# Mixer output projection: one accumulation over eight feature tiles in place of six and then two

## The chip, the core and the metric

The kernel runs on one core of a Trainium2 chip. Its time is the time of one launch on the device, in microseconds (us). The core has a matrix engine (TensorE, "PE" in the profile), an engine for elementwise work on two tensors (VectorE, "DVE"), one for functions of one tensor (ScalarE, "ACT"), a slower elementwise engine (GpSimd, "POOL") and one that issues the transfers (SyncE, "SP"). Each engine works through its own queue in order; engines wait for each other by semaphores.

## The reference, cut to what matters

One decoder layer over 1,024 prompt tokens and 32 sample tokens, 1,056 in all, all in float32. The part that matters here stands between the mixer and the second feed-forward block:

```python
merged = (sigmoid(gate_s5) * (y_s5 @ w_s5_up) + sigmoid(gate_m) * (hm @ w_m_up))
x = x + merged @ w_out                                   # w_out is 1024 x 1024
x = x + 0.5 * swiglu(rmsnorm(x, g_ffn2), w2_gate, w2_up, w2_down)
```

## The kernel before

Activations lie with features on the 128 partitions and the 1,056 tokens along the row, so a tensor of 1,024 features is eight tiles of 128 x 1056, numbered 0 to 7. Tokens go in three column pieces, `CH`: 384, 384 and 288. Float32 accuracy is had by splitting each operand into a high and a low part and multiplying three times (high by high, high by low, low by high: `mm3`, lines 109 to 111). `split` (lines 92 and 93) makes the parts: a copy on ACT gives the high one, a subtraction on DVE the low one. `weight` loads a block of weights (line 100) and splits it; `unit` accumulates one output piece of 128 x 384 or 128 x 288 over a list of feature tiles in one bank of PSUM, of which the tag "mm" has four.

`join` first makes the eight merged tiles `mg` (high and low, sixteen tiles), from the products `mm_mu`. Then comes the output projection `mm_wo`, which the change touches. It runs in two passes: for each of the eight output tiles, a product over the feature tiles 0 to 5, added to the residual tile `x` by `piece` (line 1297, on DVE); and then, again for each output tile, a product over the feature tiles 6 and 7, added in the same way. Only behind the second of these is a tile of `x` complete, and `hook(m)` is called.

The hook is that of `norm_s`. It prepares the second feed-forward block and has this work:

- for every tile of `x`, three squares on ACT (lines 339 and 342) and their sum on DVE (line 343, into `rb_n`);
- for every second tile, `build`: a store of the two tiles of `x` to DRAM (line 332), scaled copies `n3na` and `n3nb` on ACT (lines 326 to 328), four sums on POOL (`forms`, lines 135 to 138, written over the two tiles of `x`), and seven splits into the forms `n3b11`, `n3t3`, `n3t2`, `n3t1`, `n3b21`, `n3t4`, `n3nb22` of a fast matrix multiplication (`sproducts`): seven copies on ACT and seven subtractions on DVE. The program has four builds, 0 to 3;
- behind the last tile, for each of the three column pieces, `rstd`: a product `nps_n` on PE, a few tiny operations on DVE with a power on POOL (line 305) between them, a product `nrb_n` on PE, and a copy on ACT.

After this the feed-forward block starts. Its products `mma` and `mmd` can be run up to a point while the hook's work is going on; `mmb` (line 183) stands in PE's queue behind the last `nrb_n`. From `mmb` on PE is kept busy.

Two stores of tiles matter. All tiles of 128 x 1056, `x`, `mg` and the seven forms of each build among them, come from one pool of 34 slots (tag "s"); a tile whose slot isn't free yet waits for the last reader of the one that held it. `n3na` and `n3nb` come from a pool of two. The split weights come from a pool of eight (tag "w"), four pairs.

Nothing in the kernel fixes the order of the queues, apart from a few loads that are pinned: a scheduler orders each engine's instructions when the program is built, by priority and by its own estimate of when things become ready.

Of the kernel before, what the change touches and what calls it, by code (L numbers as in the profile page):

```python
# [10 lines left out]
ALU = mybir.AluOpType  # L11
# [4 lines left out]
P = 128  # L16
# [3 lines left out]
KT = 8  # L20
# [10 lines left out]
CH = ((0, 384), (384, 384), (768, 288))  # L31
# [4 lines left out]
class Kernel:  # L36
# [1237 lines left out]
    def join(self, hook):  # L1274

        nc, v, a = self.nc, self.nc.vector, self.a
        hm = self.hm
        mg = self.new_hl(2, "mg") + self.new_hl(4, "mg2", "x") + [tuple(self.ph.tile([P, NT], F32R, tag="s", name=f"mg{q}{k}") for q in "hl") for k in (6, 7)]
        for m in range(KT):
            w = self.weight(a["w_m_up"][0][:, m * P:(m + 1) * P], f"mu{m}")  # L1280
            tm = self.pr.tile([P, RW], F32, tag="r", name=f"jm{m}")[:, :NT]
            self.pinned_load(tm, self.d_tm[m])
            for j, (o, n) in enumerate(CH):
                ps = self.unit(w, hm, j, f"mu{m}_{j}")
                t = self.pt.tile([P, 384], F32, tag="h", name=f"mg{m}_{j}")[:, :n]
                v.scalar_tensor_tensor(t, tm[:, o:o + n], 1.0, ps, op0=ALU.add, op1=ALU.mult)
                v.tensor_tensor(t, t, self.a5[m][:, o:o + n], ALU.add)
                self.split(t, mg[m][0][:, o:o + n], mg[m][1][:, o:o + n])
        self.x = [self.pa.tile([P, NT], F32, tag="s", name=f"x2_{m}") for m in range(KT)]
        for m in range(KT):  # L1290
            self.pinned_load(self.x[m], self.d_x[m])

        def piece(w, ks, m, c, j):
            o, n = CH[j]
            ps = self.unit(w, ks, j, f"wo{m}_{j}_{len(ks)}", c)
            xs = self.x[m][:, o:o + n]
            v.scalar_tensor_tensor(xs, ps, 0.25, xs, op0=ALU.mult, op1=ALU.add)
        wo = a["w_out"][0]
        for m in range(KT):
            w = self.weight(wo[:6 * P, m * P:(m + 1) * P], f"wo{m}")  # L1300
            for j in range(3):
                piece(w, mg[:6], m, 0, j)
        ws = [self.weight(wo[6 * P:, 512 * i:512 * i + 512], f"wo_{i}") for i in range(2)]
        for m in range(KT):
            for j in range(3):
                piece(ws[m // 4], mg[6:], m, m % 4, j)
            hook(m)


# [140 lines left out]
```

## Time and profile before

| | us |
|---|---|
| median of three runs | 2322.53 |
| lowest and highest run | 2320.86, 2325.98 |
| the profiled execution | 2326.38 |
| its span, first to last instruction | 2324.7 |

The span is what the trace shows, and all positions below are microseconds from its start. The profiled execution took 1.7 us more than its span. PE is busy for 2252.8 us of it. The output projection, with the hook's work behind it, lies from about 1535 to 1673 us. Names in the trace leave the numbers of tiles out, so `x` stands for any of the eight tiles.

### The profile page before, as it was taken

How to read it: one execution, taken by the hardware profiler on the slowest of the kernel's cores; microseconds unless marked ns; L12 is line 12 of the kernel's file. 1: busy time of each engine (PE TensorE's matmuls, PEld its weight loads, DVE VectorE, ACT ScalarE, POOL GpSimd, SP SyncE). 2: the span in 40 equal slices, each digit the busy share in tenths (PEclk: the TensorE clock that was granted, in tenths of full speed). 3: DMA queues.
4: the chain of work that ended last, by engine and by line, in shares of the span. 5: the costliest groups of instructions: out<-in, count | busy, mean ns of one | idle time of the engine just before them, and what ended most of it. 6: DMA issues, size and time to landing. Idle time of an engine off the chain costs nothing.

```text
span 2324.7 us, 39749 instructions
## 1 busy us (share of the span) xinstructions
PE 2252.8 (97%) x15663; PEld 2206.2 (95%) x15663; DVE 1394.2 (60%) x3211; ACT 823.7 (35%) x1560; POOL 549.1 (24%) x570
## 2 busy tenths in 40 slices
PE   5999999999999999999999999999699999999999
PEld 4899999999999999999999889999599999999998
DVE  5655555335858867769676476535755555523754
ACT  6433333113424433444344252213533333311543
POOL 4676664000001100000000000002576766100000
PEclk8899999999999999999999999999799999999999
DMA  5122226421444542122124676232123222722101
GB/s 196 56 74 67 82 74 198 145 74 46 142 122 121 138 136 60 53 65 63 52 60 128 179 269 251 84 130 75 51 74 92 74 77 91 252 72 69 56 19 75
DMA packets 283492, 240.48 MB, mean 103 GB/s; under 512 B 28652, under 2 KB 260044, under 8 KB 283304
## 3 DMA queue, kind: packets, MB, share of 16 engines
q1 hardware_dynamic: 264064, 216.34, 30.2%
q10 hardware_dynamic: 19240, 21.59, 2.8%
q8 instruction: 123, 2.02, 0.4%
q14 instruction: 65, 0.53, 0.1%
HBM read 168.04 MB, written 67.35 MB: 101 GB/s over the span
## 4 chain that ended last, share of the span: by engine, by line
PE 88%; DVE 6%; DMA 2%; issue 1%; ACT 1%; POOL 1%; SPq 1%; DVEq 0%; ACTq 0%; POOLq 0%
PE mm_qk L110 3%; PE mm_qk L109 3%; PE mm_qk L111 3%; PE mm_f2d L110 2%; PE mm_f1d L110 2%; PE mm_f2d L111 2%; PE mm_f1d L111 2%; PE mm_f2d L109 2%; PE mm_f1d L109 2%; PE mmc_f2g L183 2%; PE mmc_f2u L183 2%; PE mmd_f2u L183 2%; PE mmd_f1u L183 2%; PE mma_f2u L183 2%; PE mma_f1u L183 2%; PE mmc_f1u L183 2%
## 5 line engine op out<-in xcount | busy, mean ns | idle before, releaser
L109 PE MATMUL mm_qk<-n2h,wh_qk 128*128 128x384 f32 (+1 forms) x384 | 125.9, 328 | 0.0
L110 PE MATMUL mm_qk<-n2l,wh_qk 128*128 128x384 f32 (+1 forms) x384 | 125.8, 327 | 0.0
L109 PE MATMUL mm_f1d<-f1hh,wh_f1d 128*128 128x384 f32 (+1 forms) x384 | 122.8, 326 | 2.6 <-DVE x_f L415 1.5
L111 PE MATMUL mm_qk<-n2h,wl_qk 128*128 128x384 f32 (+1 forms) x384 | 125.3, 326 | 0.0
L110 PE MATMUL mm_f1d<-f1hl,wh_f1d 128*128 128x384 f32 (+1 forms) x384 | 124.6, 325 | 0.4 <-DVE f1hl L93 0.4
L109 PE MATMUL mm_f2d<-f2hh,wh_f2d 128*128 128x384 f32 (+1 forms) x384 | 123.1, 326 | 1.8 <-ACT f2hh L92 1.5
L110 PE MATMUL mm_f2d<-f2hl,wh_f2d 128*128 128x384 f32 (+1 forms) x384 | 124.0, 324 | 0.7 <-DVE f2hl L93 0.7
L111 PE MATMUL mm_f1d<-f1hh,wl_f1d 128*128 128x384 f32 (+1 forms) x384 | 124.5, 325 | 0.0
L111 PE MATMUL mm_f2d<-f2hh,wl_f2d 128*128 128x384 f32 (+1 forms) x384 | 123.5, 322 | 0.0
L1014 POOL TENSOR_TENSOR cy<-cs,mhalf 128x1 f32<-128x1 f32 x32 | 20.3, 635 | 431.4 <-DVE cs L1013 408.4
L305 POOL TENSOR_TENSOR rc_n<-nv_n,mhalf 128x3 f32<-128x3 f32 x12 | 13.5, 1126 | 425.8 <-DVE nv_n L301 397.1
L415 DVE SCALAR_TENSOR_TENSOR x_f<-mm_f1d,x_f 128x384 f32<-128x384 f32 (+1 forms) x72 | 37.0, 520 | 88.0 <-PE mm_f1d L111 87.7
L956 DVE SCALAR_TENSOR_TENSOR cv<-raw,vecs,cv 128x384 f32<-128x384 f32 (+1 forms) x144 | 84.8, 589 | 7.3 <-ACT cv L954 6.1
L415 DVE SCALAR_TENSOR_TENSOR x_f<-mm_f2d,x_f 128x384 f32<-128x384 f32 (+1 forms) x72 | 37.1, 520 | 85.6 <-PE mm_f2d L111 85.6
L158 POOL TENSOR_TENSOR wr_f2g<-wr_f2g,wr_f2g 128x512 f32<-128x512 f32 x16 | 20.6, 1287 | 242.9 <-DVE wa_f2g L93 233.7
L109 PEld LDWEIGHTS mm_f1d<-f1hh,wh_f1d 128*128 128x128 f32 x384 | 72.4, 189 | 3.3 <-DVE x_f L415 1.7
L109 PEld LDWEIGHTS mm_f2d<-f2hh,wh_f2d 128*128 128x128 f32 x384 | 71.7, 188 | 2.9 <-ACT f2hh L92 2.1
L110 PEld LDWEIGHTS mm_f2d<-f2hl,wh_f2d 128*128 128x128 f32 x384 | 72.1, 188 | 1.3 <-DVE f2hl L93 1.3
L110 PEld LDWEIGHTS mm_f1d<-f1hl,wh_f1d 128*128 128x128 f32 x384 | 72.7, 189 | 0.6 <-DVE f1hl L93 0.6
L111 PEld LDWEIGHTS mm_f1d<-f1hh,wl_f1d 128*128 128x128 f32 x384 | 72.7, 189 | 0.0
L110 PEld LDWEIGHTS mm_qk<-n2l,wh_qk 128*128 128x128 f32 x384 | 72.3, 188 | 0.1
L111 PEld LDWEIGHTS mm_qk<-n2h,wl_qk 128*128 128x128 f32 x384 | 72.2, 188 | 0.1
(728 smaller groups left out, 7501.2 us busy)
## 6 DMA issues: line engine op xcount, KB each, us to landing
d_xs<-x SPq DMA_DIRECT2D x16, 528.0 KB
d_f1h<-f1h SPq DMA_DIRECT2D x16, 528.0 KB
f1hr<-d_f1h SPq DMA_DIRECT2D x16, 528.0 KB
x_f<-d_xs SPq DMA_DIRECT2D x16, 528.0 KB
d_f2h<-f2h SPq DMA_DIRECT2D x16, 528.0 KB
f2hr<-d_f2h SPq DMA_DIRECT2D x16, 528.0 KB
wr_f1g<-in_w_gate_dram SPq DMA_DIRECT2D x16, 512.0 KB
wr_f1u<-in_w_up_dram SPq DMA_DIRECT2D x16, 512.0 KB
```

What stands on the lines that cost most here:

```text
L109: mm(ps, wh, xh, start=start, stop=False)
L110: mm(ps, wh, xl, start=False, stop=False)
L111: mm(ps, wl, xh, start=False, stop=stop)
L158: g.tensor_tensor(src, src, add, ALU.add)
L183: nc.tensor.matmul(ps, w[:, wq, i], f[q][:, xq, cs], start=start and i == j == 0, stop=i == n - 1 and j == 2, skip_group_check=not start)
L305: nc.gpsimd.tensor_tensor(r, ms, self.mhalf[:, :nt], ALU.pow)
L415: v.scalar_tensor_tensor(xs, ps, 0.5, xs, op0=ALU.mult, op1=ALU.add)
L956: v.scalar_tensor_tensor(acc, raw[:, o + i:o + i + wd], self.cw[:, i, T:T + 1], acc, op0=ALU.mult, op1=ALU.add)
L1014: nc.gpsimd.tensor_tensor(y, ss, self.mhalf[:n, 0:1], ALU.pow)
```

## The change

The two passes become one: for each output tile, a weight block of all 1,024 rows is loaded and split, one product runs over all eight feature tiles, one update adds it to `x`, and the hook is called at once.

```diff
         for m in range(KT):
-            w = self.weight(wo[:6 * P, m * P:(m + 1) * P], f"wo{m}")
-            for j in range(3):
-                piece(w, mg[:6], m, 0, j)
-        ws = [self.weight(wo[6 * P:, 512 * i:512 * i + 512], f"wo_{i}") for i in range(2)]
-        for m in range(KT):
-            for j in range(3):
-                piece(ws[m // 4], mg[6:], m, m % 4, j)
+            w = self.weight(a["w_out"][0][:, m * P:(m + 1) * P], f"wo{m}")
+            for j, (o, n) in enumerate(CH):
+                ps = self.unit(w, mg, j, f"wo{m}_{j}")
+                xs = self.x[m][:, o:o + n]
+                v.scalar_tensor_tensor(xs, ps, 0.25, xs, op0=ALU.mult, op1=ALU.add)
             hook(m)
```

The number of matrix products stays as it was (8 x 3 x 8 x 3). Updates of `x` go from 48 to 24, weight blocks from ten (eight of 128 x 768, two of 128 x 1024) to eight of 128 x 1024. The scheduler orders everything from here to the start of the feed-forward block anew.

On ACT, before the change, all weight blocks of the projection (`wh_wo`) and the first four of the feed-forward block stand ahead of the first square of the hook (`rb_n3` from `x2_0`):

```order
L92 ACTIVATE wh_wo3_16997<-wr_wo3_16995 128x768
L92 ACTIVATE mgh7_15995<-mg7_2_16776 128x288
L92 ACTIVATE wh_wo4_17063<-wr_wo4_17061 128x768
L92 ACTIVATE wh_wo5_17129<-wr_wo5_17127 128x768
L92 ACTIVATE wh_wo6_17195<-wr_wo6_17193 128x768
L92 ACTIVATE wh_wo7_17261<-wr_wo7_17259 128x768
L92 ACTIVATE wh_wo_0_17327<-wr_wo_0_17325 128x1024
L92 ACTIVATE wh_wo_1_17333<-wr_wo_1_17331 128x1024
```

Now, at the same place of ACT's queue, the hook of tile 0 stands between the weight blocks 3 and 5:

```order
L92 ACTIVATE wh_wo3_17104<-wr_wo3_17102 128x1024
L92 ACTIVATE mgh7_15995<-mg7_2_16776 128x288
L339 ACTIVATE rb_n3_15979<-x2_0_16781 128x384
L339 ACTIVATE rb_n3_15979<-x2_0_16781 128x384
L92 ACTIVATE wh_wo4_17229<-wr_wo4_17227 128x1024
L339 ACTIVATE rb_n3_15979<-x2_0_16781 128x288
L326 ACTIVATE n3na_0_16979<-x2_0_16781,vecs_144 128x1056
L92 ACTIVATE n3b11_0_16988<-n3na_0_16979 128x528
```

The hook's ACT work for the tiles 0 to 6 is spread in this way over the whole projection.

Later in ACT's queue, where the last output tile (7) is made, now stand the seven copies of build 2 between the squares of tile 7, and behind them the first scaled copy of build 3 (`n3na_3`):

```order
L342 ACTIVATE sq_n30_7_17622<-x2_7_16788 128x384
L92 ACTIVATE n3b11_2_17424<-n3na_2_17415 128x528
L92 ACTIVATE n3t3_2_17427<-x2_5_16786 128x528
L92 ACTIVATE n3t2_2_17430<-x2_4_16785 128x528
L342 ACTIVATE sq_n31_7_17625<-x2_7_16788 128x384
L92 ACTIVATE n3t1_2_17433<-x2_4_16785 128x528
L92 ACTIVATE n3b21_2_17436<-n3nb_2_17416 128x528
L92 ACTIVATE n3t4_2_17439<-x2_5_16786 128x528
L92 ACTIVATE n3nb22_2_17442<-n3nb_2_17416 128x528
L326 ACTIVATE n3na_3_17633<-x2_6_16787,vecs_144 128x1056
```

These seven tiles take the slots of `mg` tiles: the program gives them the addresses of the high and low parts of the feature tiles 0 to 3. The builds 0 and 1 lie ahead of this, in slots that were free or held finished tiles of `x`.

On POOL, behind the last output tile, the rows of build 3 (`x2_6`, `x2_7`) and of the powers (`rc_n3`) before the change had one sum of feed-forward weights (`wr0_f2u0`, line 158) among them:

```order
L305 TENSOR_TENSOR rc_n3_15980<-nv_n30_17724,mhalf_88 128x3
L135 TENSOR_TENSOR x2_7_16788<-n3na_3_17693,n3nb_3_17694 128x528
L137 TENSOR_TENSOR x2_6_16787<-n3nb_3_17694,x2_6_16787 128x528
L158 TENSOR_TENSOR wr0_f2u0_18034<-wr0_f2u0_18034,wr1_f2u0_18036 128x4x128
L138 TENSOR_TENSOR x2_7_16788<-n3nb_3_17694,x2_6_16787 128x528
L305 TENSOR_TENSOR rc_n3_15980<-nv_n31_17741,mhalf_88 128x3
L305 TENSOR_TENSOR rc_n3_15980<-nv_n32_17758,mhalf_88 128x3
```

Now three stand there, and the power of the second column piece (`nv_n31`) ahead of the last sum:

```order
L305 TENSOR_TENSOR rc_n3_15980<-nv_n30_17664,mhalf_88 128x3
L136 TENSOR_TENSOR x2_6_16787<-n3na_3_17633 128x528
L158 TENSOR_TENSOR wr0_f2u0_17974<-wr0_f2u0_17974,wr1_f2u0_17976 128x4x128
L135 TENSOR_TENSOR x2_7_16788<-n3na_3_17633,n3nb_3_17634 128x528
L137 TENSOR_TENSOR x2_6_16787<-n3nb_3_17634,x2_6_16787 128x528
L158 TENSOR_TENSOR wr1_f2u0_17976<-wr1_f2u0_17976 128x4x128
L158 TENSOR_TENSOR wr0_f2u0_17974<-wr0_f2u0_17974,wr1_f2u0_17976 128x4x128
L305 TENSOR_TENSOR rc_n3_15980<-nv_n31_17681,mhalf_88 128x3
L138 TENSOR_TENSOR x2_7_16788<-n3nb_3_17634,x2_6_16787 128x528
L305 TENSOR_TENSOR rc_n3_15980<-nv_n32_17698,mhalf_88 128x3
```

Two weight sums that were done earlier have moved in among the rows of the last build.

## Rows read from the trace of the kernel before

**Rows 1.** The page: busy time by engine, and PE's clock over 40 slices.
```profile
PE 2252.8 (97%) x15663; PEld 2206.2 (95%) x15663; DVE 1394.2 (60%) x3211; ACT 823.7 (35%) x1560; POOL 549.1 (24%) x570
...
PEclk8899999999999999999999999999799999999999
```

**Rows 2.** By stretch: its length; busy PE, PEld, DVE, ACT, POOL; clock, DMA, GB/s.
```profile
1534.80:1604.10 69.30, 69.30 (x432) 69.30 (x431) 22.05 (x35) 8.07 (x10) 3.86 (x3) 1.00 0.29 98
1604.10:1632.10 28.00, 25.37 (x149) 23.31 (x148) 26.20 (x44) 17.69 (x32) 11.00 (x8) 1.00 0.35 135
1632.10:1673.00 40.90, 21.82 (x109) 18.83 (x107) 35.23 (x57) 24.59 (x45) 23.09 (x16) 0.68 0.13 46
1673.00:1680.00 7.00, 7.00 (x41) 6.96 (x41) 1.84 (x5) 2.42 (x4) 0.75 (x1) 0.67 0.00 0
```

**Rows 3.** The chain that ended last, 1500 to 1700: start, us, what.
```profile
1609.60 0.56 DVE x L1297
...
1656.69 0.63 DVE n3b L93
```

**Rows 4.** Timeline of PE: start, us, instruction, [idle before, releaser].
```profile
1534.85 0.34 PE L109 MATMUL mm_wo<-mgh,wh_wo 128*128 128x384 f32 x1
...
1541.14 0.30 PE L109 MATMUL mm_wo<-mgh,wh_wo 128*128 128x288 f32 x1
...
1543.53 0.33 PE L109 MATMUL mm_wo<-mgh,wh_wo 128*128 128x384 f32 x1
...
1632.02 0.88 PE L183 MATMUL mma_f2g<-n3b,wa_f2g 128*128 128x264 f32 x6
...
1673.04 3.01 PE L183 MATMUL mmb_f2g<-n3t,ws_f2g 128*128 128x264 f32 x12
...
1680.21 1.63 PE L183 MATMUL mmd_f2g<-n3t,wa_f2g 128*128 128x264 f32 x12
```

**Rows 5.** Waits of 1604 to 1680: who, for whom, us in total, times, longest.
```profile
PEld mm_wo L109 <- DVE x L1297: 4.6, 7, 1.6
```

**Rows 6.** Timeline of DVE, ACT and POOL around the builds 2 and 3.
```profile
1623.39 0.54 DVE L343 TENSOR_TENSOR rb_n<-rb_n,sq_n 128x384 f32<-128x384 f32 x1
...
1644.51 0.69 DVE L93 TENSOR_TENSOR n3b<-n3na,n3b 128x528 fp32r<-128x528 f32 x1
...
1646.43 4.40 DVE L343 TENSOR_TENSOR rb_n<-rb_n,sq_n 128x384 f32<-128x384 f32 x3 [0.39 <-ACT sq_n L342]
1647.32 1.61 POOL L137 TENSOR_TENSOR x<-n3nb,x 128x528 f32<-128x528 f32 x1
...
1649.71 1.16 ACT L326 ACTIVATE n3na<-x,vecs 128x1056 f32<-128x1056 f32 x1
...
1653.34 0.63 ACT L92 ACTIVATE n3nb<-n3nb 128x528 fp32r<-128x528 f32 x1
1653.87 0.63 ACT L92 ACTIVATE n3b<-n3na 128x528 fp32r<-128x528 f32 x1
...
1656.00 0.69 DVE L93 TENSOR_TENSOR n3nb<-n3nb,n3nb 128x528 fp32r<-128x528 f32 x1
1656.62 0.69 DVE L93 TENSOR_TENSOR n3b<-n3na,n3b 128x528 fp32r<-128x528 f32 x1
...
1657.37 0.72 ACT L328 ACTIVATE n3nb<-x,nvecs 128x528 f32<-128x528 f32 x1
...
1661.37 1.68 POOL L158 TENSOR_TENSOR wr_f2u<-wr_f2u,wr_f2u 128x512 f32<-128x512 f32 x1 [0.62 <-DVE ws_f2u L93]
...
1661.91 1.70 DVE L93 TENSOR_TENSOR n3t<-x,n3t 128x528 fp32r<-128x528 f32 x1
```

**Rows 7.** Timeline of SP, POOL and DVE around build 0.
```profile
1607.98 16.67 SPq L332 DMA_DIRECT2D d_xs<-x  x5
...
1610.92 1.87 POOL L136 TENSOR_TENSOR x<-n3na 128x528 f32<-128x528 f32 x1 [9.16 <-ACT sq_n L342]
...
1628.44 0.70 DVE L93 TENSOR_TENSOR n3nb<-n3nb,n3nb 128x528 fp32r<-128x528 f32 x1
```

More of the change, by code (lines that the diff above doesn't have):

```diff
@@ L1291, in join @@
             self.pinned_load(self.x[m], self.d_x[m])
[L1293 to L1298, printed above, removed]
-        for m in range(KT):
-            w = self.weight(wo[:6 * P, m * P:(m + 1) * P], f"wo{m}")
-            for j in range(3):
-                piece(w, mg[:6], m, 0, j)
-        ws = [self.weight(wo[6 * P:, 512 * i:512 * i + 512], f"wo_{i}") for i in range(2)]
-        for m in range(KT):
-            for j in range(3):
-                piece(ws[m // 4], mg[6:], m, m % 4, j)
+        for m in range(KT):
+            w = self.weight(a["w_out"][0][:, m * P:(m + 1) * P], f"wo{m}")
[3 more added lines that the diff above has]
+                v.scalar_tensor_tensor(xs, ps, 0.25, xs, op0=ALU.mult, op1=ALU.add)
             hook(m)
```

## The prediction, made before the changed kernel was run

> **What bounds the kernel now.** I read the page first. PE is busy 97% of the span, and its clock stands at 9 tenths or more in all slices but three: the first two and the one from 1627 to 1685 us [rows 1]. So the kernel is bound by PE, and the one soft place in the middle is where the change stands. The busy time by stretch shows why [rows 2]. In the first pass of the output projection (1534.8 to 1604.1) PE is full and the others rest: DVE works 22.05 of 69.3 us, ACT 8.07, POOL 3.86. In the second pass DVE works 26.20 of 28.0 us. Behind it, up to 1673.0, PE has gaps, and DVE works 35.23 of 40.9 us. The chain of waits agrees: from 1609.60 to 1657.3 it runs on DVE with hardly a break [rows 3]. The reader is to see two halves that don't overlap: while PE multiplies, the hook's work (squares, builds) can't begin, since no tile of `x` is complete before the second pass; and when that comes, eight tiles are completed in 28 us, and DVE has more to do than it can. PE pays twice. In the second pass it waits for DVE to empty its PSUM banks (4.6 us in 7 waits [rows 5]); after it, it waits for the builds and the norm, from 1632.02, when the last product of the projection is issued, to 1673.04, when `mmb` starts [rows 4]: 41.0 us, the tail.
>
> **The change, part by part.** The numbers are against the profiled execution, 2326.38 us, which is 3.85 us above the median of the three runs; I carry the difference over to the median at the end.
>
> First, the projection on PE. The number of products is the same. An output tile with 54 of them takes 1543.53 - 1534.85 = 8.68 us [rows 4], so one with 72 takes 11.57, and eight of them 92.6. The projection would end at 1534.85 + 92.6 = 1627.4, which I call T0, in place of 1632.02: a gain of 4.6 us. It is the waits of rows 5. A product of 24 matmuls lasts 24 x 0.133 = 3.2 us in the short piece ((1543.53 - 1541.14) / 18 [rows 4]) and more in the others, against 1.0 us or less for one with six, and there are four banks, so an update has some 10 us before PE waits for it. Half of the 48 updates go as well; before, the first pass hid half of them, and the other half is part of DVE's load in the second.
>
> Second, the hook moves. Tile m is now complete about 11.6 x (m + 1) us after the start. All squares and sums but those of tile 7, and the builds 0 and 1 whole, now lie beside PE's products. What hides them: DVE, ACT and POOL were idle there for 47, 61 and 65 of 69.3 us [rows 2]. Their transfers move along: the stores of `x` now stand among the weight loads on SP (the store of tile 0 ahead of the load of weight block 7, that of tile 1 ahead of the first weights of the feed-forward block), so those loads wait for the update of a tile. A weight's slot comes free three output tiles (34.7 us) before the weight is used, and that is the cover; if it went, PE would stand still for what is late (the slower rival, below).
>
> Third, what is left behind T0. The forms of build 2 take the slots of `mg`, so its first copy must wait until the last product piece has read feature tile 0: three of its 24 matmuls, that is T0 - 3.2 + 0.4 = T0 - 2.8. I walk along ACT's queue from there, with the times from rows 6: seven copies by 0.53 (1653.34 to 1653.87), a square 0.4, the scaled copy `n3na_3` 1.1, two weight copies 1.1, a square 0.4, one copy 0.5, and two halves of `n3nb_3` 1.4. This ends at T0 + 5.8. DVE has seven subtractions by 0.62 (1656.00 to 1656.62) and two others meanwhile, and is through with build 2 at T0 + 3.3, in time for `n3nb_3`, which takes over a buffer of build 2. POOL's sum over tile 7 must also wait for the store of that tile; at build 0 POOL started 2.9 us after the issue of the store [rows 7], so this is done by T0 + 4 and is covered.
>
> From the end of `n3nb_3` the same steps follow as before: POOL's sums, the last splits, the powers, `nrb_n`, `mmb`. Before, they took 1673.04 - 1658.09 = 14.95 us [rows 4, 6]. But two sums of feed-forward weights now stand among them in POOL's queue that used to be done earlier, at 1.68 us each [rows 6]: 3.4 us. The tail becomes 5.8 + 14.95 + 3.4 = 24.1 us, in place of 41.0: a gain of 16.9.
>
> A second way to the same term: from the first subtraction of build 2 (1644.51 [rows 6]) to `mmb` it took 28.5 us before, and that subtraction would now be at T0 - 2.1, which gives 26.4. I take 24.1, since its longest leg is the same work without tile 7's sums in it, and keep the other for the range.
>
> The tail's unknown is how DVE and POOL get in each other's way. Three sums beside POOL's work took 4.40 us, one alone took 0.54, and a subtraction that began within a POOL sum took 1.70 in place of 0.69 [rows 6]; so a POOL sum costs a DVE operation about 1 us. The low bound is a tail in which two such meetings and the weight sums cost nothing: 24.1 - 2 - 3.4 = 18.7. The high bound is the second estimate with the two weight sums on top: 26.4 + 3.4 = 29.8.
>
> The Trainium skill (SBUF — State Buffer, Who interferes with whom) says that a DVE instruction with two SBUF inputs and a GpSimd instruction that reads SBUF exclude each other for the whole instruction; the rows above agree. By that rule, DVE could lose the most of a POOL sum (1.6 to 1.9 us) at each meeting, and with some four meetings more than I count the tail would be about 28; without it, it would be near the low bound.
>
> The clock is the other unknown. Over the tail the granted clock averages 0.68, and over the seven microseconds behind it 0.67, between the two levels of 1.2 and 2.4 GHz, where the first pass has 1.00, the upper one [rows 2]; PE had stood still for half of the tail before. Twelve `mmb` products take 3.01 us there, twelve `mmd` at 1680.21, at full clock, 1.63 [rows 4]. With 41 matmuls in those 7 us, at 0.12 each, about 2 us are lost. Smaller gaps may give them back: 0 to 2 us; I take 0.
>
> The sum: 4.6 + 16.9 = 21.5 us; 2326.4 - 21.5 = 2304.9. Against the median, 2322.5 - 21.5 = 2301.
>
> **Rivals.** (a) The tail doesn't shrink: build 2 and build 3 can't begin before the end of the projection, because `mg` holds its sixteen slots to the end, whereas before the twelve of the first six feature tiles came free at 1604. For it: the two late builds are those that the chain ran through. Against it: of DVE's 35.23 us in the old tail, the two builds are 14 subtractions by 0.69, some 10 us; the rest (sums of the tiles 3 to 7, build 1) is done before T0. If it holds nonetheless, only the 4.6 us of the projection remain: 2318. The Trainium skill (Perfetto Trace Analysis, Identifying Performance Opportunities) warns that regular gaps on the engine that should be full can mean that there is no room for the next tile; by that, the gaps would stay where they were.
>
> (b) What is gained is partly given back: the feed-forward block starts some 20 us earlier, its first weights have less time to be loaded, summed on POOL and split, and PE waits for them behind `mmb`. For it: three POOL weight sums are now crammed into the tail. Against: PE still works on the gate's weights 7 us behind `mmb` [rows 4], and four of the seven forms that the up-projection needs next stand in ACT's queue ahead of the copies that end the tail. A third of the gain would go, 7 us: 2308.
>
> (c) Slower: the weights of the projection come late. The copies and subtractions of the weight blocks 4 to 7 stand behind hook work in ACT's and DVE's queues, and this behind POOL's sums. Build 0 took from 1608 to 1629 before, in a crowd [rows 7]. The point from which it decides is 34.7 us; if a build held a weight up for twice what it took then, 42 us, PE would stand still for 7 us at each of the four blocks, 28 us in all, and the gain of 21.5 would be more than gone: 2329. Against: 23 us per pair of tiles, with ACT and DVE half empty.
>
> **How the numbers follow.** I give my forecast, with its bounds, 0.80; rival (b) 0.09; (a) 0.07; (c) 0.04. The forecast's own bounds are a gain of 4.6 + 41.0 - 29.8 = 15.8 (2307) to 4.6 + 41.0 - 18.7 + 2 = 28.9 (2294). The range takes in (b), the single microseconds by which runs differ, and a part of the way to (a): 2293 to 2313. About 0.2%, 4.6 us, is what a measurement of this kernel can tell from no change; (a) lies on that bound and counts half. Faster 0.92, same 0.05, slower 0.03.
>
> **What would show it.** In the changed kernel's profile the stretch of the projection is one block of some 92.6 us with PE full; `mmb` stands about 24 us behind it; DVE is busy for some 40 us within the block in place of 22. A wait of `mm_wo` for `wl_wo` or `wh_wo` would show (c); a tail of 35 us or more (a); waits for `wa_f2u` or `ws_f2u` behind `mmb`, (b). The forecast is wrong if the projection is longer than 95 us, or the tail outside 19 to 30.

## The result, and the profile after

| | before | after |
|---|---|---|
| median, us | 2321.70 (4 runs, 2320.83 to 2325.98) | 2303.39 (4 runs, 2302.52 to 2306.43) |
| the profiled execution, its span | 2326.38, 2324.7 | 2302.52, 2300.8 |

The ratio is 0.992, with a 95% interval of 0.9905 to 0.9936: 18.3 us less, where 21.5 were forecast. The time lies 2.4 us above the forecast of 2301 and inside the range.

The page after, which answers to [rows 1], shows PE busy for 10.5 us less, and the low spot of the clock at 8 in place of 7:

```profile
PE 2242.3 (97%) x15663; PEld 2199.2 (96%) x15663; DVE 1380.9 (60%) x3185; ACT 823.8 (36%) x1558; POOL 550.3 (24%) x570
...
PEclk8899999999999999999999999999899999999999
```

By stretch, with the columns of [rows 2]: the projection, the tail, and the seven microseconds behind `mmb`.

```profile
1531.50:1624.10 92.60, 92.60 (x577) 92.60 (x577) 49.81 (x74) 37.34 (x63) 23.10 (x16) 1.00 0.31 111
1624.10:1650.30 26.20, 19.00 (x111) 17.97 (x109) 18.69 (x36) 12.50 (x23) 14.40 (x10) 0.73 0.16 52
1650.30:1657.30 7.00, 7.00 (x48) 7.00 (x48) 2.69 (x7) 3.05 (x5) 1.46 (x2) 0.81 0.00 0
```

PE is full for 92.6 us, and DVE, ACT and POOL now work beside it. The tail is 26.2 us in place of 40.9, but PE still has 7.2 us of holes in it, and the clock is at 0.73, between its two levels of 1.2 and 2.4 GHz.

PE's timeline after, to compare with [rows 4]: the first product of the projection, the first instruction behind it (T0, the sums of the norm), every row of the tail that PE had to wait for, and what follows the tail.

```profile
1531.46 0.34 PE L109 MATMUL mm_wo<-mgh,wh_wo 128*128 128x384 f32 x1
...
1624.10 0.72 PE L298 MATMUL nps_n<-ones,rb_n 128*128 128x2 f32 x6
...
1632.89 1.25 PE L183 MATMUL mma_f2g<-n3b,wa_f2g 128*128 128x264 f32 x4 [3.36 <-DVE n3b L93]
...
1645.01 0.93 PE L315 MATMUL nrb_n<-ident,rc_n 128*128 128x128 f32 x6 [1.72 <-DVE rc_n L309]
1645.78 0.70 PE L298 MATMUL nps_n<-ones,rb_n 128*128 128x2 f32 x6
1648.61 1.75 PE L315 MATMUL nrb_n<-ident,rc_n 128*128 128x128 f32 x6 [2.12 <-DVE rc_n L309]
1650.29 2.94 PE L183 MATMUL mmb_f2g<-n3t,ws_f2g 128*128 128x264 f32 x12
1653.07 1.63 PE L183 MATMUL mmc_f2g<-n3t,ws_f2g 128*128 128x264 f32 x12
```

The projection takes 1624.10 - 1531.46 = 92.64 us, before 97.17; the tail 1650.29 - 1624.10 = 26.19, before 41.02. Together that is 19.36 us. From `mmb` to the end of the span it is 650.5, before 651.7: another 1.1 us, some 0.8 of it because the twelve `mmc` products behind `mmb` take 1.63 us, where before they took 2.45. The two executions differ by 3.4 us more, because the projection started at 1531.46 and not at 1534.85. This isn't credited to the change: nothing ahead of it was edited, and in the profiled executions of the kernels with four banks that start lies anywhere from 1529.3 to 1534.9.

One stretch of the tail shows what the forecast did not price. These are rows of ACT, DVE and POOL after, in order of time, as in [rows 6]:

```profile
1621.40 0.65 ACT L92 ACTIVATE n3b<-n3na 128x528 fp32r<-128x528 f32 x1 [3.30 <-PE mm_wo L110]
...
1628.10 1.32 POOL L136 TENSOR_TENSOR x<-n3na 128x528 f32<-128x528 f32 x1
1628.16 1.28 DVE L306 TENSOR_TENSOR nt_n<-rc_n 128x3 f32<-128x3 f32 x1 [0.76 <-POOL rc_n L305]
1629.17 0.72 ACT L328 ACTIVATE n3nb<-x,nvecs 128x528 f32<-128x528 f32 x1
...
1629.96 0.15 DVE L307 TENSOR_TENSOR nt_n<-nt_n,nv_n 128x3 f32<-128x3 f32 x1
...
1630.80 1.41 POOL L158 TENSOR_TENSOR wr_f2u<-wr_f2u,wr_f2u 128x512 f32<-128x512 f32 x1 [1.38 <-DVE wa_f2u L93]
1631.01 1.23 DVE L308 TENSOR_SCALAR nt_n<-nt_n 128x3 f32<-128x3 f32 x1
...
1632.17 1.84 POOL L135 TENSOR_TENSOR x<-n3na,n3nb 128x528 f32<-128x528 f32 x1
1632.77 1.26 DVE L309 TENSOR_TENSOR rc_n<-rc_n,nt_n 128x3 f32<-128x3 f32 x1
```

The first copy of build 2 (`n3b`, 1621.40) starts at T0 - 2.7, and the last scaled copy of build 3 (`n3nb`) ends at 1629.89, T0 + 5.8, both as forecast. The four DVE operations on 128x3 are one step of the row norm (`rstd`). The one that meets no POOL work takes 0.15 us; the other three take 1.23 to 1.28, and each ends within 0.03 us of the end of the POOL operation that it met. They stand in DVE's queue among the splits: the split for which PE waited 3.36 us came behind the third of them, and `nrb_n` needs the last. Before the change all four took 0.15 or 0.16 us. These are the first and the last of them there, and the first two `nrb_n`:

```profile
1655.24 0.15 DVE L306 TENSOR_TENSOR nt_n<-rc_n 128x3 f32<-128x3 f32 x1
...
1657.42 0.16 DVE L309 TENSOR_TENSOR rc_n<-rc_n,nt_n 128x3 f32<-128x3 f32 x1
...
1658.41 1.48 PE L315 MATMUL nrb_n<-ident,rc_n 128*128 128x128 f32 x6
...
1667.80 0.93 PE L315 MATMUL nrb_n<-ident,rc_n 128*128 128x128 f32 x6 [1.02 <-DVE rc_n L309]
```

So this step took 1657.58 - 1655.24 = 2.3 us before and takes 1634.03 - 1628.16 = 5.9 now. It is the first of three (one for each column piece); the eight small operations of the other two take 0.15 to 0.17 us in both kernels.

### The profile page after: what moved, and what is told of

Read it like the earlier page. It is cut to its first block, busy times and chain, and to the rows that moved or that the text cites. A ratio compares the mean times of both kernels' runs of the same rounds, so it can differ in the third digit from the quotient of the medians.

```text
span 2300.8 us, 39729 instructions
## 1 busy us (share of the span) xinstructions
PE 2242.3 (97%) x15663; PEld 2199.2 (96%) x15663; DVE 1380.9 (60%) x3185; ACT 823.8 (36%) x1558; POOL 550.3 (24%) x570
## 4 chain that ended last, share of the span: by engine, by line
PE 89%; DVE 4%; DMA 3%; issue 2%; SPq 1%; POOL 1%; ACT 1%; POOLq 0%; DVEq 0%; ACTq 0%
PE mm_qk L110 3%; PE mm_qk L109 3%; PE mm_qk L111 3%; PE mm_f2d L110 2%; PE mm_f2d L111 2%; PE mm_f2d L109 2%; PE mm_f1d L110 2%; PE mm_f1d L111 2%; PE mm_f1d L109 2%; PE mma_f2g L183 2%; PE mma_f2u L183 2%; PE mmd_f1u L183 2%; PE mmd_f2u L183 2%; PE mmc_f2g L183 2%; PE mmc_f2u L183 2%; PE mma_f1u L183 2%
## 5 line engine op out<-in xcount | busy, mean ns | idle before, releaser
L109 PEld LDWEIGHTS mm_qk<-n2h,wh_qk 128*128 128x128 f32 x384 | 72.3, 188 | 0.0
```

What stands on the lines that cost most here:

```text
L109: mm(ps, wh, xh, start=start, stop=False)
```

## The experiments

All of them start from the changed kernel, apart from the first (passes of two and six) and the last, which start from the kernel before. "Tail" is the time from the first instruction behind the projection to the first `mmb`, in the profiled execution.

| | projection | tail | median, us | ratio to before, 95% |
|---|---|---|---|---|
| before | 97.17 | 41.0 | 2321.7 to 2323.8 | |
| after | 92.64 | 26.2 | 2303.39 | 0.9905 to 0.9936 |
| passes of two and six | 92.76 | 25.1 | 2302.66 | 0.9895 to 0.9924 |
| last two tiles in halves | 92.66 | 26.8 | 2303.41 | 0.9895 to 0.9928 |
| build 3's sums on DVE | 92.64 | 25.7 | 2300.97 | 0.9886 to 0.9916 |
| weight sums on DVE | 92.64 | 24.7 | 2301.56 | 0.9888 to 0.9918 |
| both of these | 92.64 | 23.5 | 2299.91 | 0.9887 to 0.9916 |
| norm in one piece | 92.64 | 19.4 | 2302.64 | 0.9901 to 0.9934 |
| one piece, sums on DVE | 92.63 | 22.1 | 2299.58 | 0.9887 to 0.9917 |
| no row norm | 92.64 | | 2288.49 | 0.9839 to 0.9868 |
| norm shares banks | 92.64 | | 2290.37 | 0.9848 to 0.9877 |
| norm behind four products | 92.64 | | 2293.26 | 0.9858 to 0.9887 |
| a bank for the norm alone | | | 2322.51 | 0.9986 to 1.0005 |
| before, norm shares banks | 97.18 | 23.5 | 2311.04 | 0.9928 to 0.9961 |

In the kernels with shared banks PE works ahead of and behind `mmb`, so the place of `mmb` says little there. What can be compared is the time from the first instruction behind the projection (T0) to the end of the span: 692.7 us before, 676.7 after, 665.3 with shared banks, 667.1 with the norm behind four products, 672.9 with a bank for the norm alone.

**Is it the single accumulation, or that tiles are completed one by one?** The two passes are kept, with their 48 updates, but swapped, so that the second pass is the long one. The edit is against the kernel before; its removed lines are left out here.

```diff
+        ws = [self.weight(wo[:2 * P, 512 * i:512 * i + 512], f"wo_{i}") for i in range(2)]
         for m in range(KT):
+            for j in range(3):
+                piece(ws[m // 4], mg[:2], m, m % 4, j)
+        for m in range(KT):
+            w = self.weight(wo[2 * P:, m * P:(m + 1) * P], f"wo{m}")
+            for j in range(3):
+                piece(w, mg[2:], m, 0, j)
             hook(m)
```

> The passes of the kernel before in the other order: first a product over the feature tiles 0 and 1 for all output tiles, then one over 2 to 7 with the hook behind each output tile. Still 48 updates, ten weight blocks and two passes. Theory (the gain is that tiles of x are completed one by one, 8.7 us apart, so that the hook's work lies beside products): the long pass is a full block of about 69.5 us, the tail from the last product of the projection to mmb is 20 to 27 us, the time 2298 to 2307 us. Rival (the gain is the deeper accumulation: fewer updates, no short products that wait for PSUM): 2315 us or more, near the kernel before.

It took 2302.66 us, with a tail of 25.1, as the theory has it: the whole gain, with no deeper accumulation and no fewer updates. What pays is that an output tile is completed every 8 to 12 us and not every 3.5, so the hook's work lies beside PE's.

**Do the slots of `mg` set the length of the tail?** The last two output tiles are made in halves, 6a, 7a, 6b, 7b, so that half of `mg` is free earlier. The lines added, in part:

```diff
+        steps = [(m, 0, 8) for m in range(6)] + [(6, 0, 4), (7, 0, 4), (6, 4, 8), (7, 4, 8)]
+        for m, lo, hi in steps:
...
+            for j in range(3):
+                piece(ws[m], lo, hi, m, j)
+            if hi == 8:
+                hook(m)
```

> The changed kernel, but the last two output tiles are each made in two products over four feature tiles, in the order 6 first half, 7 first half, 6 second half, 7 second half, so that eight slots of mg come free 11.6 us before the end of the projection. Theory (build 2 is held behind the end by the slots): build 2 is done before the last product, the tail falls from 26.2 to 16 to 21 us, the time is 5 to 10 us under the changed kernel's, 2293 to 2299. Rival (the tail is set by POOL's chain behind the last tile of x, and the slots don't matter): a tail of 25 to 27 us and 2302 to 2305.

The copies of build 2 started 12.7 us before the end of the projection, in place of 2.7 (ACT's first is shown below). The tail stayed, at 26.8 us, and the time too, as the rival has it. So the slots set when build 2 starts, as the prediction says, but not when `mmb` starts. In this kernel POOL and DVE meet four times in a row, at the norm (two of the four meetings, and the PE row that waited for the last):

```profile
1610.69 0.65 ACT L92 ACTIVATE n3b<-n3na 128x528 fp32r<-128x528 f32 x1 [8.23 <-PE mm_wo L110]
...
1631.35 1.29 POOL L135 TENSOR_TENSOR x<-n3na,n3nb 128x528 f32<-128x528 f32 x1
1631.41 1.24 DVE L306 TENSOR_TENSOR nt_n<-rc_n 128x3 f32<-128x3 f32 x1 [0.76 <-POOL rc_n L305]
...
1635.09 1.26 POOL L158 TENSOR_TENSOR wr_f2u<-wr_f2u,wr_f2u 128x512 f32<-128x512 f32 x1
1635.18 1.18 DVE L309 TENSOR_TENSOR rc_n<-rc_n,nt_n 128x3 f32<-128x3 f32 x1
...
1636.42 1.65 PE L315 MATMUL nrb_n<-ident,rc_n 128*128 128x128 f32 x6 [4.91 <-DVE rc_n L309]
```

The norm had taken the place of the build as the last thing to be ready.

**What is POOL's part?** Three kernels put sums on DVE: the four sums of build 3, the sums of the first up-projection weights (`f2u0`), and both. The two edits:

```diff
     def forms(self, i, fill, tmp, name):
         nc, v, g = self.nc, self.nc.vector, self.nc.gpsimd
+        if name == "n3" and i == 3:
+            g = v
...
     def sweights(self, src, name):
         nc, pw, g, v = self.nc, self.pw, self.nc.gpsimd, self.nc.vector
+        if name == "f2u0":
+            g = v
```

> The changed kernel with the four sums of build 3 on DVE in place of POOL. Theory (in the tail DVE and POOL hold each other up, and POOL's sums at 1.3 to 1.8 us are on the path): the tail falls from 26.2 to 20 to 23 us, the time to 2297 to 2300. Rival (DVE alone is what is full in the tail): four more operations at 0.62 us on DVE, a tail of 28 to 29 us, 2305 to 2306.

> The changed kernel with the four sums of the first up-projection weights of the feed-forward block (three of them in the tail) on DVE in place of POOL. By the prediction's term (two weight sums that moved in among POOL's rows cost 3.4 us): the tail falls from 26.2 to 21 to 24 us, the time to 2298 to 2301. Rival (they are hidden, or DVE pays for them as much): 26 to 28 us and 2303 to 2306.

> The four sums of build 3 and the sums of the first up-projection weights run on DVE, none on POOL, so that in the tail POOL has little but the powers. Theory C (128x3 operations of the norm take 1.2 us in place of 0.15 because POOL works beside them): they fall to under 0.3 us wherever POOL stands still, the first norm piece comes 3 us earlier, against which DVE has some 8 sums of 0.55 to 0.7 us more; net a tail of 22 to 25 us, 2299 to 2303. If POOL is not the reason, the small operations stay at 1.2 us and the tail grows to 27 or more by the added sums: 2304 or more.

They measured 25.7, 24.7 and 23.5 us of tail. The first lies between its theory and its rival, in tail and in time. So does the second, nearer to its theory: the weight sums, priced at 3.4 us, give back 1.5 when they move to DVE. The intervals of all three overlap that of the changed kernel, so what is said of POOL here rests on the rows of the small operations and not on these few microseconds. In the kernel with both edits POOL has only the powers left, and all twelve of the small operations take 0.15 to 0.17 us, as these rows of DVE show:

```profile
1628.91 0.16 DVE L310 TENSOR_TENSOR nt_n<-rc_n 128x3 f32<-128x3 f32 x1 [0.76 <-POOL rc_n L309]
1630.56 0.15 DVE L311 TENSOR_TENSOR nt_n<-nt_n,nv_n 128x3 f32<-128x3 f32 x1
1631.85 0.16 DVE L312 TENSOR_SCALAR nt_n<-nt_n 128x3 f32<-128x3 f32 x1
1633.76 0.15 DVE L313 TENSOR_TENSOR rc_n<-rc_n,nt_n 128x3 f32<-128x3 f32 x1
```

So POOL is what stretched them. But the step still takes 5.0 us (1628.91 to 1633.91) in place of 5.9, since DVE now has the sums in between. The tail is 2.7 us shorter and the median 3.5, within theory C's numbers.

**Is it the norm's three pieces?** They are joined to one piece of nine columns; and, in a second kernel, this is combined with the sums on DVE.

```diff
-                for j, (o, n) in enumerate(CH):
-                    self.rstd(j, st["rb"][:, o:o + n], st["rc"], st["rb"], name)
+                self.rstd_once(st["rb"], st["rc"], name)
...
+        for i in range(9):
+            nc.tensor.matmul(ps[:rows(i), 2 * i:2 * i + 2], rb[:, i * P:i * P + rows(i)], self.ones, start=True, stop=True)
...
+        nc.gpsimd.tensor_tensor(rc, ms, self.mhalf, ALU.pow)
```

> The three row-norm pieces (one per column piece: sums to PSUM, small DVE operations, a power on POOL, a Newton step on DVE, a broadcast on PE) are done as one piece of 9 columns. Theory A (the norm's chain of three pieces through the in-order queues sets the tail): two of three passes through PE, DVE and POOL go, mmb comes 17 to 21 us behind the end of the projection in place of 26.2, and the time falls by 5 to 9 us to 2294 to 2298. Theory B (the forms of build 2 and 3 and the PE products behind them set it, as the prediction had it): the tail stays at 25 to 27, the time at 2302 to 2305.

> Both edits, the norm in one piece and the sums on DVE. Theory A with C: each pays for itself, a tail of 16 to 20 us, 2293 to 2297. Theory B: no better than the sums on DVE alone, 2299 to 2303.

This is undecided. The profiled execution had a tail of 19.4 us and took 2296.47, as theory A has it, at a mean granted clock of 0.991; its three other executions took 2302.36, 2304.85 and 2302.92, as theory B has it, at 0.988 to 0.989, and have no trace. With the sums on DVE the tail was 22.1, outside theory A's range, and the median that of the sums alone, as theory B has it. PE still waits for one broadcast of all pieces in both.

**What is left without the norm?**

```diff
-            if m == KT - 1:
-                for j, (o, n) in enumerate(CH):
-                    self.rstd(j, st["rb"][:, o:o + n], st["rc"], st["rb"], name)
```

> Leaves out the row norm of the second feed-forward block altogether (its square sums stay, the scales are not formed), to see what the tail is without its chain. Theory A: builds and products alone need 14 to 18 us from the end of the projection to mmb, so 8 to 12 us less than 26.2, 2291 to 2296. Theory B: the tail stays within 2 us of 26.2, 2301 to 2304.

This kernel leaves out the scales of the norm, so it doesn't compute the layer; only its time is of use. 2288.49 us: 14.9 less than the changed kernel, more than either theory had. The norm's own products on PE account for some 4 to 5 of it (three groups of sums by 0.7 us and three broadcasts by 0.8 to 0.9, as PE's rows at full clock have them in the kernel with shared banks below). PE's timeline, from its first instruction behind the projection on, shows where the rest comes from:

```profile
1623.96 1.01 PE L183 MATMUL mma_f2g<-n3b,wa_f2g 128*128 128x264 f32 x7
...
1626.15 1.26 PE L183 MATMUL mmb_f2g<-n3t,ws_f2g 128*128 128x264 f32 x9
1627.25 1.26 PE L183 MATMUL mmc_f2g<-n3t,ws_f2g 128*128 128x264 f32 x9
```

`mmb` starts 2.2 us behind T0. The operands of its first nine products were ready by then. What it stood behind in PE's queue in the changed kernel was `nrb_n`, and no data joins the two. They share a pool of four PSUM banks: the norm takes six tiles of it (`nps` and `nrb` of three pieces), then `mmb` and `mmc` follow. That gave a new theory: banks are handed out in the order of the program, so `mmb` cannot have one before the last `nrb` has. The trace after has this order at every piece of the norm: the sums of the second piece come directly behind the first broadcast (below), those of the third behind the second broadcast, and `mmb` behind the third (both in the rows of PE further up). Here the second sums run 11.4 us behind T0; in the kernel with shared banks below it is 2.9.

```profile
1634.08 1.65 PE L315 MATMUL nrb_n<-ident,rc_n 128*128 128x128 f32 x6
1635.52 1.28 PE L298 MATMUL nps_n<-ones,rb_n 128*128 128x2 f32 x6
```

**Three tests of the banks.** First: the sums and the broadcast of a piece share one bank, so that the norm needs three tiles.

```diff
...
+        if name == "n3":
+            bank = self.pv.tile([P, 512], F32, tag="aux", name=f"nbk_{name}{j}")
+            ps = bank[:, 384:]
...
-        ps = self.pv.tile([P, 512], F32, tag="aux", name=f"nrb_{name}{j}")[:, :n]
+        ps = (self.pv.tile([P, 512], F32, tag="aux", name=f"nrb_{name}{j}") if bank is None else bank)[:, :n]
```

> The row norm computes as before and in the same place of the program; only its sums and its broadcast of one column piece share one PSUM bank, so that it takes three banks of the pool of four that it shares with the products mmb and mmc, in place of six. Theory D (these banks are handed out in the order of the program, so mmb can't start before the norm's last broadcast has got its bank, and PE has nothing else to do): nine matmuls of mmb now stand ahead of the first broadcast in PE's queue, mmb starts 10 to 14 us behind the end of the projection in place of 26.2, and 5 to 9 us go: 2294 to 2298. Theory A' (the norm's chain itself is what later work waits for, since every gate needs its scales): the idle time only moves behind mmb, 2301 to 2304.

Second: on top of this, the norm stands in the program behind the first four products.

```diff
         product(e, 3, True)
+        if mid:
+            mid()
         put(1, 1, e, w3, ALU.add)
...
```

> The norm's pieces (each with one bank) stand in the program behind the first four products of the feed-forward block, so that those come first to banks and queues. Without the norm altogether the time was 2288.5; its 18 small matmuls on PE take about 5 us. Theory D: mmb starts within 6 us of the end of the projection, PE idles under 5 us in all, 2292 to 2297. Theory A': 2300 or more, with PE idle for DVE's rc or ACT's rb behind the products.

Third: the norm has a bank of its own, and the pool has three.

```diff
-        self.pv = pool("paux", 4, space=PSUM)
+        self.pv = pool("paux", 3, space=PSUM)
...
+            bank = self.pv.tile([P, 512], F32, tag="nrm", name=f"nbk_{name}{j}", bufs=1)
...
```

> The norm has a PSUM bank of its own, for all three pieces in turn, and the pool that it shared has three banks in place of four, in the whole program. Theory D: mmb starts within 6 us of the end of the projection and the tail's idle time goes, 8 to 11 us less there; against it stand the other stages with three banks, for which the traces have no row: 0 to 10 us. 2292 to 2303. Theory A': no gain in the tail, 2303 to 2313.

In the queue of PE as the program sets it, `mmb` came behind the last `nrb_n` in the changed kernel:

```
L315 MATMUL nrb_n32_17711<-ident_81,rc_n3_15980 128x128 x2
L315 MATMUL nrb_n32_17711<-ident_81,rc_n3_15980 128x32
L183 MATMUL mmb_f2g0_0_17778<-n3t2_0_16994,ws2_f2g0_17731 128x264 x3
```

With shared banks nine of its products come directly behind the last sums, ahead of every broadcast:

```
L303 MATMUL nbk_n32_17695<-ones_86,rb_n3_15979 32x2
L183 MATMUL mmb_f2g0_0_17775<-n3t2_0_16994,ws2_f2g0_17728 128x264 x3
```

and the time is 2290.37 us, 13.0 less than the changed kernel and 3.6 better than theory D's best. The timeline of PE, from T0 (1623.00) on, with both rows for which PE waited, the sums of the second piece and the last broadcast; behind them the 30 us from T0 by stretch, in this kernel:

```profile
1625.87 0.72 PE L303 MATMUL nbk_n<-ones,rb_n 128*128 128x2 f32 x6
...
1630.10 0.76 PE L303 MATMUL nbk_n<-ones,rb_n 128*128 128x2 f32 x6 [1.00 <-DVE rb_n L348]
1630.79 1.37 PE L183 MATMUL mmb_f2g<-n3t,ws_f2g 128*128 128x264 f32 x9
...
1634.69 0.93 PE L320 MATMUL nbk_n<-ident,rc_n 128*128 128x128 f32 x6 [1.37 <-DVE rc_n L314]
...
1640.47 0.94 PE L320 MATMUL nbk_n<-ident,rc_n 128*128 128x128 f32 x6
```

```profile
1623.00:1653.00 30.00, 27.63 (x225) 27.04 (x224) 25.71 (x48) 17.56 (x33) 20.88 (x19) 1.00 0.19 63
```

and the same 30 us in the changed kernel, ahead of them its stretch from 1200 to 1500:

```profile
1200.00:1500.00 300.00, 296.06 (x1966) 282.26 (x1965) 188.34 (x481) 104.28 (x215) 5.97 (x11) 0.99 0.54 179
...
1624.10:1654.10 30.00, 22.80 (x131) 21.77 (x130) 19.49 (x38) 14.18 (x25) 14.40 (x10) 0.72 0.14 45
```

225 matmuls against 131, at a granted clock of 1.00 against 0.72. Ninety-four matmuls by 0.122 us, start to start (1654.53 - 1653.07 for twelve in the changed kernel's timeline at full clock), are 11.5 us, nearly the whole difference. PE waits for 2.4 us in place of 7.2; the rest goes with the clock, which stays at its upper level through the whole stretch. Seven of the norm's small operations still take 1.2 us beside POOL, and the kernel without the norm is only 1.9 us faster: their time hardly matters any more. One thing came along with the test: the sums of a piece no longer stand behind the broadcast of the piece before, so the norm itself is done sooner, with its last broadcast at T0 + 17.5 (1640.47) in place of T0 + 24.5 (1648.61). By itself this test doesn't tell that from `mmb` going first; the second one does. This is the fastest of the complete versions, 33 us below the kernel before; sums on DVE on top of it were not tried.

The second test came to 2293.26, within theory D's range, but behind the first: with the norm later, PE waits 2.0 and 0.7 us for its small operations. These are its first `mmb` and its last broadcast:

```profile
1626.28 1.26 PE L183 MATMUL mmb_f2g<-n3t,ws_f2g 128*128 128x264 f32 x9
...
1651.54 0.94 PE L322 MATMUL nbk_n<-ident,rc_n 128*128 128x128 f32 x6
```

Here the norm ends later than in the changed kernel (T0 + 27.5, with T0 at 1624.09), and still 10.1 us go. So the place of `mmb`, and of `mmc` behind it, is worth some 10 of the 13 us without a norm that ends sooner; how the other 3 divide, these runs don't show.

The third, at 2322.51, lies above the ranges of both theories. `mmb` starts 2.9 us behind T0, as theory D has it, but from T0 to the end only 3.8 us are gained, and far more is lost ahead of it. Its own stretches, 1200 to 1500 and the 30 us from T0 (1646.38):

```profile
1200.00:1500.00 300.00, 286.12 (x1855) 269.44 (x1854) 183.91 (x487) 103.91 (x221) 6.48 (x12) 0.95 0.55 174
1646.40:1676.40 30.00, 27.29 (x192) 26.24 (x191) 22.26 (x39) 15.99 (x28) 15.03 (x10) 0.89 0.15 48
```

192 matmuls in the 30 us, in place of 131 (and 225 in the first test). But the projection ended 22 us later than in the changed kernel. Much of that lies between 1200 and 1500 us, where that one has PE busy for 296.06 us at a clock of 0.99, and three banks leave 286.12 at 0.95.

**Did the banks bind before the change, too?** The kernel before, with the first edit alone.

> The kernel before the change (six features, then two), with the one edit that the norm's sums and broadcast share one PSUM bank per piece. Theory D1 (the order of the banks held mmb back in the kernel before just as much, apart from what the change moved): nine matmuls of mmb stand ahead of the broadcasts here too; 9 to 13 us go, 2310 to 2314, and the change is still worth its 20 us on top. Theory D2 (before the change the builds on DVE set the tail, and the banks came to bind only once these were out of the way): less than 4 us go, 2319 to 2323, and the change would be worth some 30 us in a kernel with free banks.

2311.04 against 2323.05 us: 12.0 us, so D1 holds. PE's timeline of this kernel, from T0 and at `mmb`:

```profile
1629.94 0.89 PE L183 MATMUL mma_f2g<-n3b,wa_f2g 128*128 128x264 f32 x6
...
1653.42 2.35 PE L183 MATMUL mmb_f2g<-n3t,ws_f2g 128*128 128x264 f32 x9
```

In [rows 4] `mmb` stood 41.0 us behind T0, here 23.5. With the banks out of the way on both sides the change is worth 2311.04 - 2290.37 = 20.7 us. The two edits add up: neither takes from the other's gain more than these medians can tell.

## Why the prediction was right, step by step

**The projection** (97.17 to 92.6) was exact: 92.64, and no wait of `mm_wo` for DVE is left, where [rows 5] had 4.6 us. The swapped passes, at 92.76, have none either, with all 48 updates: it was neither the deeper accumulation nor the halved count of updates, but that the passes which complete the tiles are long enough for DVE to keep up.

**The hook's work beside PE** was right in kind; DVE had 49.8 us of it in the projection, not some 40. It cost PE nothing.

**The tail** was forecast at 24.1 and measured 26.2, between the first estimate and the second (26.4). The first leg, ACT's walk to the end of `n3nb_3`, is exact at 5.8. The second leg, "as before from there" plus the weight sums, was put at 14.95 + 3.4 = 18.35 and took 20.4. By its broadcasts (`nrb_n`) it can be taken apart:

| us | before | after |
|---|---|---|
| end of `n3nb_3` to the first broadcast | 0.3 | 4.2 |
| first to second broadcast | 9.4 | 10.9 |
| second broadcast to `mmb` | 5.2 | 5.3 |

The last part is as before. The middle one, with one weight sum more in it, grew by 1.5. The first grew by 3.9, and that goes mostly with the first norm step, 5.9 us in place of 2.3: three of its four operations now meet POOL, at two sums of build 3 and at the other added weight sum. So the leg came out near in part by luck: the weight sums were put some 1.9 too high (3.4, where moving them gave back 1.5), and the longer norm step, some 3.5, had no term. The prediction bounded such meetings at 1 us each, which is the size found, but counted them for the range alone and not on the norm's operations. Nor did it ask what the leg is made of: it has the powers, `nrb_n` and `mmb` in a row, and `mmb` needs nothing of the norm; the order of the PSUM banks put it there, in the kernel before (12.0 us) as much as after (13.0).

**The premise on the slots of `mg`** was half right: build 2 did start at T0 - 2.7, but freeing the slots ten microseconds earlier brought nothing.

**The clock behind `mmb`**, 0 to 2 us with 0 taken, gave 1.1.

**The rivals.** (a), a tail that does not shrink for want of slots, did not come; and the late halves show that its slots were not the limit of what remained either. The rule that stood beside it (the Trainium skill, Perfetto Trace Analysis, Identifying Performance Opportunities: regular gaps on the engine that should be full can mean that there is no room for the next tile) points the right way all the same, though the three gaps here (3.4, 1.7 and 2.1 us) are not one gap repeated: the room that lacked was in PSUM, not in the slots, and giving it took PE's waiting from 7.2 us to 2.4. (b): PE waits for nothing in the 110 us behind `mmb` in the trace after, and the stretch from there is shorter, not longer. (c): no wait for projection weights.

Of the 23.9 us between the two profiled executions, 4.5 are the projection, 14.8 the tail, 1.1 what is behind it, and 3.4 the start of the projection, which the change does not touch. The sum of the first three, 20.5, is what the forecast of 21.5 answers to.

## What to carry to other kernels

Work that hangs on finished tiles should be fed by tiles that are finished one at a time, at the pace of the engine that makes them; how deep each accumulation goes hardly mattered here. When a leg of a chain "takes as long as before", ask what it is made of: find for the instruction at its end what it really needs, and if its operands have long been there, look at the buffers handed out ahead of it. Here letting two tiles live in one PSUM bank gave 13 us beside the change's 18 to 21, while taking a bank away from the shared pool cost some 22 us in the stages ahead.

## What the runs showed of the hardware that was not expected

- A DVE operation on 128x3 takes 0.15 to 0.17 us alone and 1.18 to 1.28 when it meets a POOL sum (1.3 to 1.8 us), until the end of that sum. Three of the four in a step read two operands in SBUF; for these the rule of the Trainium skill (SBUF — State Buffer, Who interferes with whom), that such an operation and a GpSimd read of SBUF exclude each other for the whole instruction, agrees with the rows. The fourth (L308) has one tensor operand and was held in the same way, 1.23 us; the same section says that an instruction with one input does not contend outside the two-port modes, which it says a `tensor_scalar` can enter; in which mode this one ran no row shows.
- POOL pays as well: its power on 128x3 takes 0.86 us alone (1646.82 in the changed kernel) and 1.89 beside splits on DVE (1626.24).
- The projection's start, ahead of which nothing was edited, lay anywhere from 1529.3 to 1534.9 us in the profiled executions of the kernels with four banks. A difference of two single executions can carry up to 5.5 us of this, so stages were compared from their own start.
